# Gate, up and the sums of w_down: a written order on VectorE, ScalarE and SyncE's DMA queue

## The chip, the cores and the metric

One core of one Trainium2 chip. The metric is the device time of one execution in microseconds (us). The kernel before takes 1179.62 us, the median of three executions (1178.41 to 1179.66).

## The reference, cut to what matters

One layer with 1024 frames of width 1024: a mixer of attention and a recurrent unit, and then the part that the change touches, a SwiGLU of inner width 2816:

```python
h2 = rmsnorm(x, norm2_g[l])
x = x + (jax.nn.silu(h2 @ w_gate[l]) * (h2 @ w_up[l])) @ w_down[l]
```

All of it is float32. The kernel writes every float32 operand as a high and a low part, and every product as three products of those parts.

## The kernel before, in words

**Where the change lies.** The mixer comes first, and the diff does not touch it. After the second norm the kernel has h2, transposed, as four blocks B11, B12, B21 and B22 (512 of width by 512 frames). The 2816 columns of w_gate and of w_up are taken in 11 pairs of 128-column tiles. The first pair is multiplied the plain way, in eight blocks of 24 matmuls (`classic`). The other ten pairs are 20 steps (`Step`), in turn gate and up: g1, u1, g2, u2, up to g10, u10. A step is a 2x2 block product after Strassen and Winograd with seven products, 0 to 6, of 12 matmuls each, 84 in all. Its weight-side operands are sums of blocks of the raw weights (S1 to S4, on GpSimd in `Step.sums`), and its other side are B blocks or the sums T1 to T4 (`t_sums`, `t_split`), which are made once ahead of the steps.

**What follows each product.** `Step.run` issues product i, then what takes its result out of PSUM, then `after(i)`. Products 0, 1 and 2 are copied out by ScalarE (L1140: `pug` in a gate step, `puu` in an up step). Products 3 to 6 go through `result`: in a gate step VectorE adds a copy to the PSUM bank (L1133) and ScalarE applies silu (L1135); in an up step VectorE adds (L1128) and multiplies with the gate (L1130). Three PSUM banks, x, z and w, serve a step: products 0, 2, 4 and 6 go to x, so product 4 can't start before ScalarE has copied x after product 2, and product 6 not before VectorE has read x after product 4. Gate and up steps use different banks. `after(i)` then makes operand i of the next step (`make`, `split`): ScalarE rounds to the high part (L72, such as `au14h`: step u1, operand 4), VectorE subtracts it for the low part (L73, `au14l`). Raw weights (`graw`, `uraw`) are loaded one step ahead of that (`load_raw`).

**w_down's sums.** The last stage multiplies with w_down, also after Strassen and Winograd, in seven products P1 to P7 of 11 accumulation steps (77 steps, operands `d00h` to `d761l`, L1382). It needs four sums of w_down's blocks, and these are made in the shadow of gate and up. For each of 11 tiles f, `load_wd` issues two DMAs from ScalarE's queue (L1048, `act.dma_start`, 512 KB each) into one tile of 128 x 4 x 512 (`wd`, a pool with one buffer), `sum_wd` makes four subtractions of 128x512 on VectorE (L1054), and after the fourth SyncE's queue writes the tile to the scratch tensor `td` (L1056, 1 MB). The next `load_wd` reuses the one buffer, so its DMA waits for that write. In the code `load_wd(f)` stands after product 13f-1 and the sums 7 to 10 products behind it, so f comes every 13 products.

**What sets the order.** The framework's scheduler orders each engine's instructions by its own model of time and by priority: nothing in gate and up binds it to the written order. An engine issues its instructions in that order, one behind the other, and a DMA's issue is an instruction of the engine whose queue it uses. All other DMAs (raw weights, spills `gd` and `sd` of the gated product, `td`, and the loads of the last stage `dv`, `dx`, `dh..`, `dk`, `dq`, `dr`, `ds` in `load_d`, L1210) are issued by SyncE. In the last step, u10, `after` calls `end_step`, which issues the first loads of the last stage and makes its first operands.

Of the kernel before, what the change touches and what calls it, by code (L numbers as in the profile page):

```python
# [9 lines left out]
F32 = mybir.dt.float32  # L10
# [9 lines left out]
P = 128  # L20
# [14 lines left out]
def hymba_layer(ctx: ExitStack, tc: tile.TileContext, x, norm1_g, w_in, q_norm_g, k_norm_g, b_f,  # L35
# [5 lines left out]
    act, dve, pool, pe, sp = nc.scalar, nc.vector, nc.gpsimd, nc.tensor, nc.sync  # L41
# [9 lines left out]
    def slot(tag, name, dt=F32, shape=(P, 1024)):  # L51
        return sl.tile(list(shape), dt, tag=tag, name=name)
# [7 lines left out]
    def bank(tag, name):  # L60
        return psp.tile([P, 512], F32, tag=tag, name=name, bufs=BANKS[tag])
# [3 lines left out]
    def any_bank(name, tags=("st", "st", "st", "o", "o", "mx")):  # L65
        cyc[0] += 1
        return bank(tags[cyc[0] % len(tags)], name)

    def split(src, h, l, gain=None):

        if gain is None:
            act.copy(out=h, in_=src)  # L72
            dve.tensor_sub(out=l, in0=src, in1=f32(h))  # L73
        else:
            act.activation(out=h, in_=src, func=AF.Copy, scale=gain)
            dve.scalar_tensor_tensor(out=l, in0=src, scalar=gain, in1=f32(h), op0=ALU.mult, op1=ALU.subtract)  # L76

    def rstd(out_t, ss, n, neghalf):

        dve.tensor_scalar(out=out_t, in0=ss, scalar1=1.0 / n, scalar2=EPS, op0=ALU.mult, op1=ALU.add)  # L80
        pool.tensor_tensor(out=out_t, in0=out_t, in1=neghalf, op=ALU.pow)
# [240 lines left out]
    def sumsq_to_rstd(sq, dst, n, ps, b0=0, b1=NB):  # L322
        for b in range(b0, b1):
            pe.matmul(ps[:, b:b + 1], sq[:, b * P:(b + 1) * P], ones1[:, 0:1], start=True, stop=True)
        rstd_newton(dst[:, b0:b1], ps[:, b0:b1], n, b1 - b0)

    with tc.tile_pool(name="pp", bufs=1) as pp:
# [114 lines left out]
        for g, src in ((0, w_a), (1, w_x)):  # L442
            for o in range(2):
                sp.dma_start(out=wgr[o * HD:(o + 1) * HD, g, :, o * HD:(o + 1) * HD],
                             in_=src[0].rearrange("(t two) d e -> two d t e", two=2)[o])
# [397 lines left out]
    for h in range(H):  # L843
# [13 lines left out]
        steps = att_steps(h)  # L857
# [43 lines left out]
    NPR = NFT // 2  # L901
# [24 lines left out]
    def load_raw(nm, n):  # L926
        src = w_gate if nm == "g" else w_up
        for j in range(2):
            raw = slot("v%d" % (2 * (nm == "u") + j), f"{nm}raw{n}{j}", F32, (P, 4, 256))
            sp.dma_start(out=raw, in_=src[0, j * 512:(j + 1) * 512, n * 256:(n + 1) * 256].rearrange("(k p) c -> p k c", p=P))  # L930
            raws[nm, j] = raw
# [53 lines left out]
    with tc.tile_pool(name="nz", bufs=1) as nz:  # L985
        g2 = nz.tile([P, D], F32, name="g2")
        sp.dma_start(out=g2, in_=norm2_g[0:1, :].broadcast_to([P, D]))
        for b in range(4, NB):
            sp.dma_start(out=x1[b], in_=x1d[b * P:(b + 1) * P, :])
        x2d = dr.tile([S, D], F32, name="x2d")  # L990

        def norm2_block(b):
            xn = nz.tile([P, D], F32, tag="xn", name=f"x2n{b}", bufs=1)
            act.activation(out=xn, in_=x1[b], func=AF.Square, accum_out=ss2[:, b:b + 1])
            rstd(rs2[:, b:b + 1], ss2[:, b:b + 1], D, neghalf[:, 0:1])
            dve.scalar_tensor_tensor(out=xn, in0=x1[b], scalar=rs2[:, b:b + 1], in1=g2, op0=ALU.mult, op1=ALU.mult)
            ts = slice((b % 4) * P, (b % 4 + 1) * P)
            for kg in range(4):
                ps = any_bank(f"t2{b}{kg}", A4)
                for j in range(2):  # L1000
                    kc = kg * 2 + j
                    pe.transpose(ps[:, j * P:(j + 1) * P], xn[:, kc * P:(kc + 1) * P], ident)
                h, l = (t[kg % 2][:, :, ts] for t in B[kg // 2, b // 4])
                split(ps[:, :256].rearrange("p (k t) -> p k t", k=2), h, l)

        for b0, nb in ((0, 2), (2, 1), (3, 1), (4, 1), (5, 1), (6, 1), (7, 1)):
            groups = [(any_bank(f"wa{b}{half}", B4), b, half) for b in range(b0, b0 + nb) for half in range(2)]
            mm_out(groups)
            if b0 in (0, 3):
                sumsq_to_rstd(sqA, rsA, AW, bank("tr", f"ssA{b0}"), *((0, 4) if b0 == 0 else (4, 8)))  # L1010
            for ps, b, half in groups:
                dve.scalar_tensor_tensor(out=x1[b][:, hs(half)], in0=ps, scalar=rsA[:, b:b + 1], in1=x1[b][:, hs(half)], op0=ALU.mult, op1=ALU.add)
            for b in range(b0, b0 + nb):
                sp.dma_start(out=x2d[b * P:(b + 1) * P, :], in_=x1[b])
            for b in ((0, 1) if b0 == 2 else (b0 - 1,) if b0 else ()):
                norm2_block(b)
            if b0 == 5:
                load_raw("g", 0)
                load_raw("u", 0)
            if b0 == 6:  # L1020
                classic_ops(0)
        g_tiles(0)


        seq = ("o1 g00 N7 ta0 g10 rw tb0 ta1 g11 tb1 ta2 g01 tb2 ta3 mk0 u00 tb3 mk1 u01 mk2 u10 sp0 mk3 mk4 u11 mk5 sp1 "
               "mk6 wd0").split()
        i7 = seq.index("N7")
        for q in seq[:i7]:
            classic_ops(1) if q == "o1" else classic(q[0], int(q[1]), int(q[2]), ops0)
        norm2_block(7)  # L1030

    tz = ctx.enter_context(tc.tile_pool(name="tz", bufs=1))
# [5 lines left out]
    ND = NFT // 2  # L1038
    TD = {"T1": 0, "T3": 1, "T4": 2, "T2": 3}
    td = dr.tile([ND, P, 4, 512], F32, name="td")  # L1040
    sd = dr.tile([ND, P, 512], F32, name="sd")
    wds = {}

    def load_wd(f):
        wds[f] = wd = tz.tile([P, 4, 512], F32, tag="wd", name=f"wd{f}", bufs=1)
        for i in range(2):
            rows = slice((ND * i + f) * P, (ND * i + f + 1) * P)
            act.dma_start(out=wd[:, 2 * i:2 * i + 2, :], in_=w_down[0, rows, :].rearrange("p (j c) -> p j c", j=2))  # L1048

    def sum_wd(f, m):  # L1050

        wd = wds[f]
        o, a, b = ((0, 1, 0), (1, 3, 1), (3, 3, 0), (2, 2, 3))[m]
        dve.tensor_sub(out=wd[:, o, :], in0=wd[:, a, :], in1=wd[:, b, :])  # L1054
        if m == 3:
            sp.dma_start(out=td[f], in_=wd)  # L1056

    T1 = slots4("q", "T1")
    T2 = slots4("k", "T2")
# [8 lines left out]
    def t_sums(k):  # L1068

        if k % 2 == 0:  # L1070
            t = tz.tile([P, 4, 512], F32, tag="wd", name=f"ts{k}", bufs=1)
            u = [t[:, i, :] for i in range(4)]
        else:
            u = [temp(f"ts{k}{i}") for i in range(4)]
        for i, blk_ in enumerate((B11, B12, B21, B22)):
            h, l = ck(blk_, k)
            dve.tensor_add(out=u[i], in0=f32(h), in1=f32(l))
        for o, x_, y_ in ((0, 1, 0), (1, 3, 1), (3, 3, 0), (2, 2, 3)):
            dve.tensor_sub(out=u[o], in0=u[x_], in1=u[y_])
        tsum[k] = u  # L1080
# [74 lines left out]
    for q in seq[i7 + 1:]:  # L1155
# [4 lines left out]
        elif q == "rw":  # L1160
            load_raw("g", 1)
            load_raw("u", 1)
            steps = [Step(nm, n) for n in range(1, NPR) for nm in "gu"]
# [91 lines left out]
    def end_step(i):  # L1255
        if i == 0:
            load_d("A11", 0, places("v2", "v3"))
            load_d("B11", 0, places("v0", "v1"))
            load_d("A11", 4, places("x3"))
            load_d("B11", 4, places("x2"))  # L1260
            for n in range(3):
                source(n)
        elif i == 1:
            load_d("A11", 6, places("hE"))
            load_d("B11", 6, places("hD"))
        elif i == 2:
            last["k0"] = places("k0")
            load_d("A11", 10, last["k0"][:1])
            load_d("B11", 10, last["k0"][1:])
            load_d("B21", 0, places("hC"))  # L1270
        elif i == 3:
            load_d("A12", 0, places("k1", "k2", "k3", "q0"))
        elif i == 4:
            load_d("B21", 8, places("q2"))
        elif i == 5:
            load_d("A12", 8, places("q1"))
            load_d("S3", 0, places("r0", "r1", "r2", "r3"))
        if i < 6:
            operand(i // 2, i % 2)

    for k, st in enumerate(steps):
        def after(i):
            f, m = divmod(7 * k + i + 1, 13)
            if 0 <= f < ND:
                if m == 0:
                    load_wd(f)
                elif 7 <= m < 11:
                    sum_wd(f, m - 7)
            if k + 1 < len(steps):
                steps[k + 1].make(i)  # L1290
            else:
                end_step(i)
        if st.n + 1 < NPR:
            load_raw(st.nm, st.n + 1)
        st.run(after)

    sq2 = cp.tile([P, 2, 512], F32, tag="sqacc", name="sq2")
    hf = places("hF")
# [31 lines left out]
    for n, (nm, a_, b_, pos) in enumerate(dsteps):  # L1330
# [16 lines left out]
        if nm == "P6" and 7 <= pos < 11:  # L1347
            b = pos - 7
# [19 lines left out]
        if nm == "P4" and 4 <= pos < 8:  # L1368
            b = pos - 4
# [8 lines left out]
        for b in range(4):  # L1378
# [9 lines left out]
            u = at({"P1": x2t[0, 0], "P2": x2t[0, 0], "P3": val.get("a"), "P7": val.get("q"), "P4": val.get("q")}[nm], b)  # L1388
# [30 lines left out]
```

## Time and profile before

| what | us |
|---|---|
| three executions, median | 1179.62 |
| lowest, highest | 1178.41, 1179.66 |
| the profiled execution, its own time | 1180.42 |
| its span, first to last instruction | 1178.6 |
| TensorE busy in the span | 1144.2 |
| VectorE, ScalarE, GpSimd busy | 770.9, 536.2, 173.0 |

Span and busy times are of the profiled execution. TensorE's busy time is modelled from the ends of pipelined matmuls, so a small idle time of it is more telling than a large busy one. The mean granted clock of TensorE over the span is 0.991 of full speed.

### The profile page before, as it was taken

How to read it: one execution, taken by the hardware profiler on the slowest of the kernel's cores; microseconds unless marked ns; L12 is line 12 of the kernel's file. 1: busy time of each engine (PE TensorE's matmuls, PEld its weight loads, DVE VectorE, ACT ScalarE, POOL GpSimd, SP SyncE). 2: the span in 40 equal slices, each digit the busy share in tenths (PEclk: the TensorE clock that was granted, in tenths of full speed). 3: DMA queues.
4: the chain of work that ended last, by engine and by line, in shares of the span. 5: the costliest groups of instructions: out<-in, count | busy, mean ns of one | idle time of the engine just before them, and what ended most of it. 6: DMA issues, size and time to landing. Idle time of an engine off the chain costs nothing.

```text
span 1178.6 us, 16612 instructions
## 1 busy us (share of the span) xinstructions
PE 1144.2 (97%) x6148; PEld 969.8 (82%) x6148; DVE 770.9 (65%) x1358; ACT 536.2 (45%) x989; POOL 173.0 (15%) x152
## 2 busy tenths in 40 slices
PE   8999999998999898999989999999999999999998
PEld 6988999996888787788867887888888888888887
DVE  6436858768788775779765666654434446679693
ACT  7437867325465454454333333333333334444442
POOL 1000010012010201110522223232222100000000
PEclk9999999998999999999999999999999999999999
DMA  6021111134665466551447555533222389842320
GB/s 251 22 60 46 38 37 37 30 73 107 163 163 148 130 150 201 198 177 37 161 169 265 208 180 195 185 128 107 72 72 90 125 312 327 298 144 97 97 82 36
DMA packets 94937, 159.70 MB, mean 136 GB/s; under 512 B 13112, under 2 KB 56232, under 8 KB 93448
## 3 DMA queue, kind: packets, MB, share of 16 engines
q1 hardware_dynamic: 91688, 147.11, 39.5%
q10 hardware_dynamic: 3168, 11.54, 2.9%
q8 instruction: 48, 0.79, 0.3%
q14 instruction: 33, 0.27, 0.1%
HBM read 103.41 MB, written 38.63 MB: 121 GB/s over the span
## 4 chain that ended last, share of the span: by engine, by line
PE 75%; DVE 11%; DMA 8%; ACT 2%; issue 2%; POOL 1%; SPq 1%; ACTq 0%; DVEq 0%; POOLq 0%
PE P L1382 18%; PE Pu L965 13%; PE Pg L965 11%; PE pbv L399 4%; PE pax L383 4%; PE pbq L399 3%; PE o L727 3%; PE pag L383 3%; PE fl L812 3%; DMA td<-wd 3%; PE pbk L399 3%; PE wa L890 2%; DMA wd<-in_w_down_dram 2%; DVE wd L1054 1%; PE mx L298 1%
## 5 line engine op out<-in xcount | busy, mean ns | idle before, releaser
L713 ACT ACTIVATE pt<-st 128x512 f32<-128x512 f32 (+1 forms) x96 | 47.8, 508 | 56.8 <-PE st L708 28.5
L718 DVE TENSOR_TENSOR ringl<-pt,ringh 128x512 fp32r<-128x512 f32 (+2 forms) x96 | 58.1, 620 | 7.0 <-ACT ringh L715 5.6
L1054 DVE TENSOR_TENSOR wd<-wd 128x512 f32<-128x512 f32 x44 | 43.9, 998 | 26.0 <-DMA wd<-in_w_down_dram 25.6
L301 DVE TENSOR_REDUCE nm<-mx 128x1 f32<-128x512 f32 (+2 forms) x96 | 51.3, 551 | 13.0 <-PE mx L300 7.3
L812 PE MATMUL fl<-worec,rech 128*128 128x256 f32 x256 | 54.7, 295 | 1.9 <-DVE ql L76 1.5
L812 PEld LDWEIGHTS fl<-worec,rech 128*128 128x128 f32 x256 | 43.7, 198 | 4.4 <-DVE ql L76 1.9
L1133 DVE TENSOR_TENSOR g<-Pg,pug 128x512 f32<-128x512 f32 x30 | 20.7, 689 | 29.9 <-PE Pg L965 29.9
L705 PE MATMUL st<-set 128*128 128x512 f32 (+1 forms) x96 | 36.4, 381 | 3.6 <-ACT pt L713 3.5
L727 PE MATMUL o<-ringh,vh 128*128 128x512 f32 (+1 forms) x96 | 38.5, 401 | 0.0
L727 PE MATMUL o<-ringl,vh 128*128 128x512 f32 (+1 forms) x96 | 35.1, 366 | 2.1 <-DVE ringl L718 2.1
L812 PE MATMUL fl<-worec,recl 128*128 128x256 f32 x128 | 37.1, 290 | 0.0
L1128 DVE TENSOR_TENSOR puu<-Pu,puu 128x512 f32<-128x512 f32 x30 | 20.7, 689 | 23.3 <-PE Pu L965 23.3
L727 PE MATMUL o<-ringh,vl 128*128 128x512 f32 (+1 forms) x96 | 34.6, 360 | 0.3 <-POOL vl L679 0.3
L1135 ACT ACTIVATE g<-g 128x512 f32<-128x512 f32 x30 | 18.9, 632 | 31.0 <-DVE g L1133 21.5
L679 POOL TENSOR_TENSOR vl<-vn,vh 128x256 fp32r<-128x256 f32 x16 | 13.6, 854 | 113.5 <-ACT vh L678 113.5
L1097 POOL TENSOR_TENSOR S1g<-graw,graw 128x512 f32<-128x512 f32 x10 | 14.8, 1480 | 104.6 <-DVE T L73 34.5
L509 POOL TENSOR_TENSOR sqR<-sqR,i 128x1024 f32<-128x1024 f32 x3 | 7.2, 2405 | 152.1 <-ACT i L508 152.1
L464 DVE SCALAR_TENSOR_TENSOR xc<-xr,vcol,xc 128x1023 f32<-128x1023 f32 (+2 forms) x12 | 15.4, 1280 | 18.6 <-ACT xc L462 18.5
L298 PE MATMUL mx<-set,qms 67*128 67x512 f32 (+2 forms) x72 | 25.9, 388 | 1.3 <-DVE nm L301 1.2
L715 ACT CAST ringh<-pt 128x512 fp32r<-128x512 f32 (+1 forms) x48 | 26.4, 549 | 1.6 <-PE o L727 0.8
L890 PE MATMUL wa<-wah,atth 128*128 128x512 f32 x64 | 25.8, 403 | 0.7 <-ACT wah L72 0.7
L812 PEld LDWEIGHTS fl<-worec,recl 128*128 128x128 f32 x128 | 25.3, 198 | 0.6
(2174 smaller groups left out, 3996.8 us busy)
## 6 DMA issues: line engine op xcount, KB each, us to landing
graw<-in_w_gate_dram SPq DMA_DIRECT2D x22, 512.0 KB
uraw<-in_w_up_dram SPq DMA_DIRECT2D x22, 512.0 KB
wd<-in_w_down_dram ACTq DMA_DIRECT2D x22, 512.0 KB
gd<-g SPq DMA_DIRECT2D x22, 512.0 KB
td<-wd SPq DMA_DIRECT2D x11, 1024.0 KB
xt<-in_x_dram SPq DMA_DIRECT2D x8, 512.0 KB
set<-qh SPq DMA_DIRECT2D x16, 256.0 KB
xp<-in_x_dram SPq DMA_DIRECT2D x32, 128.0 KB
```

The source lines that it names most:

```text
L298: pe.matmul(ps[:, :w], qm[:67, qb * P:(qb + 1) * P], kb[:67, j0 * P:j0 * P + w], start=True, stop=not diag)
L301: dve.tensor_reduce(out=nm[:, ch * 8 + qb:ch * 8 + qb + 1], in_=ps[:, :nk], axis=AX.X, op=ALU.max, negate=True)
L383: pe.matmul(ps[g][:, :n], a, r, start=(kc == 0 and m == 0), stop=(kc == KC - 1 and m == 2))
L399: pe.matmul(ps[g][:, :n], a, r, start=(kc == 0 and m == 0), stop=(kc == KC - 1 and m == 2))
L713: act.activation(out=pt[:, off:], in_=ps[:, off:], func=AF.Exp)
L718: dve.tensor_sub(out=pl[:, off:], in0=pt[:, off:], in1=f32(ph[:, off:]))
L727: pe.matmul(ot[:, off:], a[:, j * VW:j * VW + P], r[:, off:], start=(j == 0 and m == 0), stop=(j == jmax and m == 2))
L812: pe.matmul(ps[:, :256], a, r, start=(n == 0), stop=(n == 11))
L890: pe.matmul(ps, a, r[:, hs(half)], start=(kc == 0 and m == 0), stop=(kc == 3 and m == 2))
L965: pe.matmul(ps, a[:, k, :], chunk(b, k), start=first and m == 0, stop=last and m == 11, skip_group_check=more)
L1054: dve.tensor_sub(out=wd[:, o, :], in0=wd[:, a, :], in1=wd[:, b, :])
L1382: pe.matmul(ps, x_[:, bs], y_, start=(begin and m == 0), stop=(end and m == 2))
```

## The change

Four things change. (1) The loop over the 20 steps is put under a manual schedule for VectorE, ScalarE and SyncE: on these three the instructions of the loop stand in the order in which the code writes them. (2) w_down's sums go by 22 units q of 256 columns, with two buffers: `load_wd(q)` stands after product 6q-3, the four sums (128x256 now) after products 6q+4 to 6q+7, and the write of 512 KB to `td` behind the fourth. The first two units are loaded ahead of the loop (`wd0 wd1`). (3) These loads are issued by SyncE, not by ScalarE. (4) `t_sums`, which borrows the same buffers, takes two tiles of half the size.

```diff
-               "mk6 wd0").split()
+               "mk6 wd0 wd1").split()
...
-    def load_wd(f):
-        wds[f] = wd = tz.tile([P, 4, 512], F32, tag="wd", name=f"wd{f}", bufs=1)
+    def load_wd(q):
+
+        f, cs = q // 2, slice((q % 2) * 256, (q % 2 + 1) * 256)
+        wds[q] = wd = tz.tile([P, 4, 256], F32, tag="wd", name=f"wd{q}", bufs=2)
         for i in range(2):
             rows = slice((ND * i + f) * P, (ND * i + f + 1) * P)
-            act.dma_start(out=wd[:, 2 * i:2 * i + 2, :], in_=w_down[0, rows, :].rearrange("p (j c) -> p j c", j=2))
-
-    def sum_wd(f, m):
-
-        wd = wds[f]
+            sp.dma_start(out=wd[:, 2 * i:2 * i + 2, :], in_=w_down[0, rows, :].rearrange("p (j c) -> p j c", j=2)[:, :, cs])
+
+    def sum_wd(q, m):
+
+        wd = wds[q]
         o, a, b = ((0, 1, 0), (1, 3, 1), (3, 3, 0), (2, 2, 3))[m]
         dve.tensor_sub(out=wd[:, o, :], in0=wd[:, a, :], in1=wd[:, b, :])
         if m == 3:
-            sp.dma_start(out=td[f], in_=wd)
+            sp.dma_start(out=td[q // 2][:, :, (q % 2) * 256:(q % 2 + 1) * 256], in_=wd)
...
-            t = tz.tile([P, 4, 512], F32, tag="wd", name=f"ts{k}", bufs=1)
-            u = [t[:, i, :] for i in range(4)]
+            t = [tz.tile([P, 4, 256], F32, tag="wd", name=f"ts{k}{i}", bufs=2).rearrange("p (a b) c -> p a (b c)", a=2) for i in range(2)]
+            u = [t[i // 2][:, i % 2, :] for i in range(4)]
...
-    for k, st in enumerate(steps):
-        def after(i):
-            f, m = divmod(7 * k + i + 1, 13)
-            if 0 <= f < ND:
-                if m == 0:
-                    load_wd(f)
-                elif 7 <= m < 11:
-                    sum_wd(f, m - 7)
...
+    with tc.manual_schedule(engines={mybir.EngineType.DVE, mybir.EngineType.Activation, mybir.EngineType.SP}):
+        for k, st in enumerate(steps):
+            def after(i):
+                e = 7 * k + i
+                for q in range(2 * ND):
+                    if e == 6 * q - 3 and q >= 2:
+                        load_wd(q)
+                    elif 0 <= e - (6 * q + 4) < 4:
+                        sum_wd(q, e - 6 * q - 4)
```

**The order in three places.** The first is ScalarE, from the end of step g1 (copies `pug`, silu into `g`) with the operands of u1 between. Before:

```order
L1140 COPY pug_6408<-Pg_6404 128x512
L72 CAST au13h<-uraw_6130 128x512
L1048 DMA wd_6668<-in_w_down_dram 128x1024
L1135 ACTIVATE g_6409<-g_6409 128x512
L72 CAST au14h<-S3u_6426 128x512
L1048 DMA wd_6668<-in_w_down_dram 128x1024
L1135 ACTIVATE g_6410<-g_6410 128x512
```

And after the change:

```order
L1142 COPY pug_6415<-Pg_6411 128x512
L72 CAST au12h<-S2u_6432 128x512
L1137 ACTIVATE g_6416<-g_6416 128x512
L72 CAST au13h<-uraw_6131 128x512
L1137 ACTIVATE g_6417<-g_6417 128x512
L72 CAST au14h<-S3u_6433 128x512
L1137 ACTIVATE g_6416<-g_6416 128x512
```

The two loads of `wd` are gone from ScalarE, and each operand's cast stands behind the result of its product, where it stood ahead of it.

The second is VectorE in step u1, where operands of g2 are made. Before:

```order
L73 TENSOR_TENSOR ag21l<-S1g_6565,ag21h 128x512
L1054 TENSOR_TENSOR wd_6942<-wd_6942 128x512
L73 TENSOR_TENSOR ag22l<-S2g_6566,ag22h 128x512
L1128 TENSOR_TENSOR puu_6549<-Pu_6548,puu_6549 128x512
L73 TENSOR_TENSOR ag23l<-graw_6402,ag23h 128x512
L1130 TENSOR_TENSOR g_6409<-g_6409,puu_6549 128x512
```

And after the change:

```order
L73 TENSOR_TENSOR ag21l<-S1g_6575,ag21h 128x512
L73 TENSOR_TENSOR ag22l<-S2g_6576,ag22h 128x512
L1130 TENSOR_TENSOR puu_6558<-Pu_6557,puu_6558 128x512
L1132 TENSOR_TENSOR g_6416<-g_6416,puu_6558 128x512
L1056 TENSOR_TENSOR wd_6402<-wd_6402 128x256
L73 TENSOR_TENSOR ag23l<-graw_6409,ag23h 128x512
```

The sum of `wd` stood ahead of the additions that empty the banks of u1; now it is half as wide, of the second unit (loaded ahead of the loop), and stands behind them.

The third is SyncE's queue at the turn to the last step, u10, with the loads of the last stage (`dv`, `dx`: first operands A11 and B11 of P1; `ds`: A22). Before:

```order
L1210 DMA dv_9204<-in_w_down_dram 128x2x512
L953 DMA gd<-g_8758 128x1024
L953 DMA gd<-g_8759 128x1024
L1210 DMA dv_9205<-in_w_down_dram 128x2x512
L1210 DMA dv_9200<-gd 128x2x512
L1210 DMA dx_9208<-gd 128x2x512
L1210 DMA dx_9210<-in_w_down_dram 128x2x512
L1210 DMA ds_9370<-gd 128x2x512
```

And after the change:

```order
L1212 DMA ds_9463<-gd 128x2x512
L1212 DMA ds_9464<-gd 128x2x512
L1058 DMA td<-wd_9088 512x1x256
L1212 DMA dv_9297<-gd 128x2x512
L1212 DMA dv_9298<-gd 128x2x512
L1212 DMA dv_9301<-in_w_down_dram 128x2x512
L1212 DMA dv_9302<-in_w_down_dram 128x2x512
L1212 DMA dx_9305<-gd 128x2x512
```

Five of the six first loads stood ahead of those of A22 and right behind the spills of u9; now all six stand behind A22's and behind the write of the last unit of `td`, which waits for its fourth sum, after product 0 of u10.

## Rows read from the trace of the kernel before

**Rows 1.** The page, busy time, share of the span, instructions: TensorE.

```profile
PE 1144.2 (97%) x6148; PEld 969.8 (82%) x6148; DVE 770.9 (65%) x1358; ACT 536.2 (45%) x989; POOL 173.0 (15%) x152
```

**Rows 2.** The chain that ended last: start, length in us, what.

```profile
946.53 19.04 PE Pu L965 x84
965.57 207.41 PE P L1382 x915
```

**Rows 3.** Instructions on the tile Pg: durations, first and last start.

```profile
L965 PEld LDWEIGHTS Pg<-B,ag10h x8: 187/188/188, 570.5 to 572.7; 128*128 128x128 f32 x8
```

**Rows 4.** Timeline of weight loads: start, us, instruction, [idle before <- releaser].

```profile
597.52 0.31 PEld L965 LDWEIGHTS Pu<-T,au12h 128*128 128x128 f32 x2 [2.62 <-ACT puu L1140]
604.90 0.30 PEld L965 LDWEIGHTS Pu<-T,au14h 128*128 128x128 f32 x2 [0.47 <-ACT puu L1140]
612.49 0.19 PEld L965 LDWEIGHTS Pu<-T4hB,au16h 128*128 128x128 f32 x1 [2.26 <-DVE puu L1128]
634.73 0.19 PEld L965 LDWEIGHTS Pg<-T4hB,ag26h 128*128 128x128 f32 x1 [3.33 <-DVE g L1133]
733.20 0.19 PEld L965 LDWEIGHTS Pu<-T4hB,au46h 128*128 128x128 f32 x1 [1.76 <-DVE puu L1128]
761.28 0.30 PEld L965 LDWEIGHTS Pu<-T,au52h 128*128 128x128 f32 x2 [1.01 <-ACT puu L1140]
```

**Rows 5.** Windows: us, busy (x instructions) by engine, clock, DMA share, GB/s.

```profile
601.00:660.00 59.00, 54.21 (x229) 43.72 (x228) 37.80 (x51) 17.26 (x30) 17.18 (x12) 0.97 0.59 214
762.00:966.00 204.00, 204.00 (x902) 168.96 (x901) 90.05 (x136) 73.93 (x127) 50.28 (x36) 1.00 0.37 123
927.00:938.00 11.00, 11.00 (x51) 9.09 (x50) 3.37 (x5) 3.94 (x7) 0.86 (x1) 1.00 0.84 285
953.00:990.00 37.00, 37.00 (x165) 30.66 (x164) 18.20 (x29) 12.86 (x23) 0.00 (x0) 1.00 0.93 330
```

**Rows 6.** Waits, 525 to 770: who for whom, us, times, longest.

```profile
DVE wd L1054 <- DMA wd<-in_w_down_dram: 25.6, 11, 7.1
...
ACT g L1135 <- DMA td<-wd: 9.5, 2, 8.1
...
ACT puu L1140 <- DMA td<-wd: 5.8, 1, 5.8
```

**Rows 7.** Timeline of ScalarE near 590.

```profile
589.91 0.33 ACTq L1048 DMA_DIRECT2D wd<-in_w_down_dram  x1
590.29 0.63 ACT L1135 ACTIVATE g<-g 128x512 f32<-128x512 f32 x1 [8.13 <-DMA td<-wd]
```

**Rows 8.** Timeline of VectorE, two sums of w_down that waited.

```profile
607.36 0.69 DVE L1054 TENSOR_TENSOR wd<-wd 128x512 f32<-128x512 f32 x1 [7.14 <-DMA wd<-in_w_down_dram]
...
626.87 0.69 DVE L1054 TENSOR_TENSOR wd<-wd 128x512 f32<-128x512 f32 x1 [4.91 <-DMA wd<-in_w_down_dram]
```

**Rows 9.** The chain again: two writes of td, 1 MB each.

```profile
598.43 4.87 DMA td<-wd
...
744.32 9.40 DMA td<-wd
```

**Rows 10.** VectorE, 128x256 once, and the 44 sums (ns least/median/most).

```profile
501.02 0.42 DVE L73 TENSOR_TENSOR B<-t,B 128x256 fp32r<-128x256 f32 x1 [0.74 <-ACT B L72]
...
L1054 DVE TENSOR_TENSOR wd<-wd x44: 676/692/1787, 574.5 to 762.0; 128x512 f32<-128x512 f32 x44
```

**Rows 11.** Timelines of SyncE and GpSimd: a raw load issued, and landed.

```profile
680.74 0.37 SPq L930 DMA_DIRECT2D uraw<-in_w_up_dram  x1
...
685.09 1.29 POOL L1097 TENSOR_TENSOR S1u<-uraw,uraw 128x512 f32<-128x512 f32 x1 [6.30 <-DMA uraw<-in_w_up_dram]
```

**Rows 12.** Timelines of VectorE, SyncE and ScalarE around the start of u10.

```profile
947.05 0.69 DVE L73 TENSOR_TENSOR au106l<-uraw,au106h 128x512 fp32r<-128x512 f32 x1 [1.91 <-ACT au106h L72]
...
931.44 0.37 SPq L1210 DMA_DIRECT2D dv<-gd  x1
...
951.83 0.62 ACT L72 CAST d01h<-dv 128x512 fp32r<-128x512 f32 x1 [1.61 <-issue]
...
955.08 0.58 ACT L1140 COPY puu<-Pu 128x512 f32<-128x512 f32 x1
```

More of the change, by code (lines that the diff above doesn't have):

```diff
@@ L1279, in end_step @@
             operand(i // 2, i % 2)
-    for k, st in enumerate(steps):
-        def after(i):
-            f, m = divmod(7 * k + i + 1, 13)
-            if 0 <= f < ND:
-                if m == 0:
-                    load_wd(f)
-                elif 7 <= m < 11:
-                    sum_wd(f, m - 7)
[L1289 to L1295, printed above, removed]
+    with tc.manual_schedule(engines={mybir.EngineType.DVE, mybir.EngineType.Activation, mybir.EngineType.SP}):
[7 more added lines that the diff above has]
+                        sum_wd(q, e - 6 * q - 4)
+                if k + 1 < len(steps):
+                    steps[k + 1].make(i)
+                else:
+                    end_step(i)
+            if st.n + 1 < NPR:
+                load_raw(st.nm, st.n + 1)
+            st.run(after)
     sq2 = cp.tile([P, 2, 512], F32, tag="sqacc", name="sq2")
```

## The prediction

> **What bounds the kernel now.** I read the page first: TensorE is busy 1144.2 of 1178.6 us [rows 1], so time can come only out of what it waits for, and a faster other engine is worth nothing by itself. Next the chain that ended last: an undisturbed step of gate and up is one row of 84 matmuls in 19.04 us, and the last stage is one unbroken run of 207.41 us [rows 2]. There is nothing to win in the last stage, nor in the late steps: from 762 to 966 TensorE is busy without a gap at clock 1.00 [rows 5].
>
> So the question is what the 20 steps take beyond 20 x 19.04 = 380.8 us. The first weight load of g1 stands at 570.5 [rows 3] and the last stage begins at 965.57 [rows 2]: 395.1 us. **The excess is 14.3 us**, and all of it lies ahead of 762. The timeline of the weight loads names it: six waits of 2.62, 0.47, 2.26, 3.33, 1.76 and 1.01 us, 11.45 in all, each ended by ScalarE's or VectorE's work on a bank [rows 4]. The other 2.8 us are matmuls that ran slower behind those waits: the granted clock is 0.97 between 601 and 660 against 1.00 later [rows 5].
>
> Why were the two engines late? The list of waits: VectorE stood 25.6 us in 11 waits for w_down's loads, ScalarE 9.5 and 5.8 us for the write of td [rows 6]. The timelines show the mechanism on both. ScalarE's next load of wd can't be issued before the one buffer is written out, and everything behind that issue stands still: silu 8.13 us, up to 590.29 [rows 7], and the copies of u1 stand behind it; TensorE waits at 597.52 and 604.90 [rows 4]. On VectorE a sum stands ahead of the additions that empty the bank and waits 7.14 us for its data at 607.36, another 4.91 at 626.87 [rows 8]; TensorE waits at 612.49 and 634.73 [rows 4]. The last of the 44 sums starts at 762.0 [rows 10], and the last gap ends at 761.28 [rows 4]: no sums, no gaps.
>
> **The change part by part.**
>
> Loads off ScalarE. 22 issues of 0.33 us [rows 7] leave it, which is off the path; what counts is that no silu, copy or cast stands behind a wait for td any more. The three waits that ScalarE ended are 2.62 + 0.47 + 1.01 = 4.1 us [rows 4], and with their share of the slow matmuls (14.3 / 11.45 = 1.25) 5.1 us.
>
> The Trainium skill ("DMA: Bandwidth & Descriptors", Issuing engines are not separate DMA queues) says that starting DMAs from several engines saves only the sequencer's time to start them, which is small. By that rule moving the loads to SyncE is worth little and those 5.1 us would stay. The rows disagree for this kernel: it is the wait ahead of the issue, 8.13 us, that ScalarE pays for.
>
> Units of 256 with two buffers. A unit is loaded after product 6q-3 and first used after 6q+4: seven products, 19.04 us. Even the slowest write of 1 MB ahead of it, 9.40 us [rows 9], and a raw load's 4.35 us from issue to landing (680.74 to 685.09) [rows 11] make 13.8. VectorE should find its data there, and the 2.26 + 3.33 + 1.76 = 7.35 us that it ended [rows 4], 9.2 with the slow share, go too. VectorE has more instructions for it: 88 sums at the 0.42 us of a 128x256 one [rows 10] are 37.0 us, where 44 at the median 0.69 are 30.4. These 6.6 us I cost at nothing: in an undisturbed step VectorE is busy 90 of 204 us [rows 5]. If that cover went, a few sums per step at 0.42 would be the price.
>
> The written order. On ScalarE and VectorE casts and low parts now stand behind the result of each product. In a gate step that makes a chain per product: add 0.69, silu 0.63, cast 0.62, subtraction 0.69 [rows 7, 8, 12] = 2.63 us, against a product of 19.04 / 7 = 2.72. It fits, and the bank that the add frees is wanted only a product later. I cost it at nothing; from above it is a few tenths per step if the links between engines add much.
>
> SyncE. It gets 44 loads of 256 KB, and 22 writes of 512 KB instead of 11 of 1 MB: 55 more issues of 0.37 us [rows 11], 20 us in 395, and it may wait for a td write ahead of each load. Behind it stand raw loads and spills. A raw load is first used a whole step and a product later, 21.8 us, and takes 4.35 [rows 11]; its two halves 8.7. So 13 us of lag cost nothing.
>
> The turn to the last stage. This is where the written order costs. The loads of the first operands of P1 stood ahead of u10: `dv` of gd was issued at 931.44 [rows 12]. Now they stand behind the last td write, which waits for au106l (947.05 + 0.69) [rows 12] and one sum of 0.42: about 948.2. ScalarE, in written order, runs copy, d00h, copy, d01h, copy; the third copy frees the bank for product 4, and stands behind d01h, which needs the third dv load, the first of B11. Four transfers of 512 KB (td, two of A11, B11), 2.1 MB, at 285 to 330 GB/s [rows 5] from about 949.5 land at 955.9 to 956.9; cast and copy, 0.62 + 0.58 [rows 12], make 957.1 to 958.1. Product 4 is due at 946.53 + 4 x 2.72 = 957.4. A lone load takes 4.35 us [rows 11], some 2.5 more than its bytes, so a landing may be up to that much later. The stall is 0 to 4 us; I take **1.0**, near the lower end, since transfers in a row hide each other's start.
>
> **The sum.** The profiled execution's own time is 1180.42 (span 1178.6 and 1.8 around it): 1180.42 - 5.1 - 9.2 + 1.0 = 1167.1. It stands 0.8 above the median of the runs, so **1166.3**.
>
> **The rivals.**
>
> 1. *Part of the early waits stays* (1173). For it: u1 comes right behind t_sums, and SyncE and VectorE still share the work; the waits of u1 are 2.62 + 0.47 + 2.26 = 5.35, 6.7 with the slow share: 1166.3 + 6.7. Against it: the releasers there all stood behind wd or td [rows 6 to 8].
> 2. *The move off ScalarE is worth nothing* (1171.4). ScalarE's three waits would stay if its copies were late for another reason than the issue ahead of them, such as the data in flight: 1166.3 + 5.1. The Trainium skill's page on DMA, cited above, would have it so. Against it: rows 7.
> 3. *The last stage starves* (1171). The six loads of dv and dx, 3.1 MB, and 0.5 MB of td come 11 us later at 330 GB/s, into a queue that was 93% busy from 953 to 990 [rows 5]. For it: all later loads shift by that. Against it: d00h to d30h are needed one after the other over 19 us, and later operands had long landed. A shift beyond the slack by 5 us gives 1171.
> 4. *SyncE's queue becomes the wait* (1186, slower). Place: the issue of a load of wd behind the td write two products (5.4 us) before. If each write takes 9.4 us [rows 9], SyncE stands 4.0 us per unit, 4.7 per step, with the raw loads behind it. It decides from 13 us per step on, as above; at 14 each of the 20 steps starts 1 us late: 1166.3 + 20. Against it: that needs three times the worst write. The Trainium skill ("DMA: Bandwidth & Descriptors", Rules for kernel authors) speaks for it: it wants 1 MiB or more per DMA, and these are halved. No run here yet shows writes in pieces of 1 KB.
> 5. *The change doesn't reach the cause* (1179.6). The waits of rows 4 would come from VectorE's load and GpSimd's, not from wd. Against it: the same steps without sums have no gap [rows 5].
>
> **How the numbers follow.** Forecast 0.73, rival 1 0.08, rival 2 0.02, rival 3 0.06, rival 4 0.05, rival 5 0.06. A measurement of this kernel can tell 0.2%, 2.4 us, from no change. Forecast and rivals 1 to 3 are faster: 0.89. Rival 5 is the same: 0.06. Rival 4 is slower: 0.05. The range: below, all 14.3 from the fastest run, 1178.41 - 14.3, some 1164.0; above, the forecast with the full 4 us of the last step is 1169.3, and rivals 2 and 3 take it to 1171.5, which leaves out rivals 1, 4 and 5, 0.19.
>
> **What the profile should show.** Right: no weight load in g1 to u9 that waits for ScalarE or VectorE; steps of 19.04 us from g1 on; no wait of ScalarE for td and hardly any of VectorE for w_down; clock 1.00 from 601 to 660; sums down to u10. In u10 d00h or d01h waits for its dv load, and product 4 perhaps for the copy behind it. Wrong: a step over 19.1 us ahead of u10, GpSimd's S1 waiting for graw or uraw, or a last stage longer than 207.4 us.

## The result, and the profile after

| | before | after |
|---|---|---|
| median of four executions, us | 1179.10 | 1166.56 |
| lowest to highest | 1178.41 to 1179.66 | 1165.24 to 1166.72 |
| profiled execution, its own time | 1180.42 | 1166.72 |
| its span | 1178.6 | 1164.9 |

The ratio is 0.9891 [0.9874, 0.9909]: the change is 12.5 us faster. The time predicted was 1166.3. One execution of the change without the order ran 1599.99 us at a mean granted clock of 0.654; it and its profile are left out below.

How the steps are measured from here on: the first weight load of g1 to the first weight load of the last stage, less the 20 x 19.04 = 380.8 us of undisturbed steps; what is left is called the steps' excess. Before, that is 570.5 [rows 3] to 965.2 (0.4 ahead of the matmul in [rows 2]), an excess of 13.9. Of the kernel after, these are two rows on tiles (duration least/median/most in ns, first and last start), the last stage and then g1:

```profile
L1386 PEld LDWEIGHTS P<-d01h,d00h x4: 188/188/188, 951.4 to 953.4; 128*128 128x128 f32 x4
L965 PEld LDWEIGHTS Pg<-B,ag10h x8: 187/188/188, 568.4 to 570.7; 128*128 128x128 f32 x8
```

951.4 - 568.4 = 383.0, an excess of **2.2 us**. So 11.7 of the 13.7 us between the two profiled executions were won in the steps; the other 2 lie ahead of g1, in work that the diff does not touch (below).

Where the steps stood still before [rows 4], the windows of the kernel after (width in us, then busy us and instructions of PE, PEld, DVE, ACT, POOL; clock; DMA share; GB/s) have no gap at all: TensorE is busy for 59.00 of 59.00 and for 373.00 of 373.00 us, at clock 1.00 where [rows 5] had 54.21 of 59 and 0.97.

```profile
601.00:660.00 59.00, 59.00 (x262) 48.84 (x261) 36.64 (x58) 20.64 (x37) 16.00 (x12) 1.00 0.50 170
568.00:941.00 373.00, 373.00 (x1647) 308.88 (x1646) 209.55 (x331) 132.72 (x235) 101.17 (x76) 1.00 0.46 153
```

What is left is in u10, two waits in the timeline of the weight loads: 0.47 us at product 5, whose first matmuls ran ahead of product 4 here, and 1.97 at product 4. They answer to [rows 4], but the releaser is now one of the last step's copies:

```profile
941.51 0.30 PEld L965 LDWEIGHTS Pu<-B,au105h 128*128 128x128 f32 x2 [0.47 <-ACT puu L1142]
944.00 0.30 PEld L965 LDWEIGHTS Pu<-T,au104h 128*128 128x128 f32 x2 [1.97 <-ACT puu L1142]
```

The chain that ended last is, as in [rows 2], the end of a step and the same unbroken 207.41 us:

```profile
944.00 7.78 PE Pu L965 x33
951.78 207.41 PE P L1386 x915
```

The busy times of the page, to be laid beside [rows 1], show that no engine has fewer instructions. TensorE has the same 6148 matmuls in 5.5 us less; part of that is the lower granted clock of before behind the waits [rows 5], the rest isn't traced. VectorE has 44 instructions and 4.2 us more:

```profile
PE 1138.7 (98%) x6148; PEld 967.0 (83%) x6148; DVE 775.1 (67%) x1402; ACT 534.8 (46%) x989; POOL 165.5 (14%) x152
```

On the tile `wd` of the kernel after, the 88 sums run from 583.1 to 932.4, where the 44 of before ran from 574.5 to 762.0 [rows 10]. In the experiments every kernel with the full gain has that spread.

```profile
L1056 DVE TENSOR_TENSOR wd<-wd x88: 409/418/1496, 583.1 to 932.4; 128x256 f32<-128x256 f32 x88
L1050 SPq DMA_DIRECT2D wd<-in_w_down_dram x44: 540/602/1485, 552.5 to 903.9; - x44
L1058 SPq DMA_DIRECT2D td<-wd x22: 562/573/596, 590.3 to 932.8; - x22
```

### The profile page after: what moved, and what is told of

It reads as the page before. It is cut to its first block, busy times and chain, and to the rows that moved or that the text cites. A ratio compares the mean times of both kernels' runs of the same rounds, so it can differ in the third digit from the quotient of the medians.

```text
span 1164.9 us, 16639 instructions
## 1 busy us (share of the span) xinstructions
PE 1138.7 (98%) x6148; PEld 967.0 (83%) x6148; DVE 775.1 (67%) x1402; ACT 534.8 (46%) x989; POOL 165.5 (14%) x152
## 5 line engine op out<-in xcount | busy, mean ns | idle before, releaser
L1056 DVE TENSOR_TENSOR wd<-wd 128x256 f32<-128x256 f32 x88 | 43.8, 498 | 0.0
L1142 ACT COPY pug<-Pg 128x512 f32<-128x512 f32 x30 | 17.6, 587 | 55.5 <-PE Pg L965 55.5
L1142 ACT COPY puu<-Pu 128x512 f32<-128x512 f32 x30 | 17.6, 587 | 45.2 <-PE Pu L965 45.2
L679 POOL TENSOR_TENSOR vl<-vn,vh 128x256 fp32r<-128x256 f32 x16 | 12.5, 791 | 112.3 <-ACT vh L678 112.3
```

The source lines that it names most:

```text
L1142: act.copy(out=(p1, p5, u1)[i], in_=ps)
```

## The experiments

The prediction had put the gain down to two parts of the change: 5.1 us to the loads that leave ScalarE, 9.2 to the units of 256 with two buffers; the written order was to be worth nothing. The rival is that the order does it, by setting the loads and sums apart. Each ratio is against the kernel before, run beside it on the same chip (its median was 1178.75 us beside the first four kernels, 1177.45 beside order and queue, early loads and the change once more, 1178.03 beside the other three), and the columns "steps" and "sums" come from one profiled execution.

| kernel | median us | ratio [95%] | steps' excess | sums, first to last start |
|---|---|---|---|---|
| written order alone | 1164.25 | 0.9879 [0.9861, 0.9898] | 0.2 | 587.0 to 950.0 |
| SyncE's queue alone | 1172.72 | 0.9949 [0.9930, 0.9967] | 8.2 | 571.4 to 746.0 |
| units and buffers alone | 1191.92 | 1.0115 [1.0092, 1.0138] | 27.2 | 571.3 to 716.1 |
| change, loads left on ScalarE | 1166.97 | 0.9901 [0.9880, 0.9921] | 1.3 | 582.2 to 931.5 |
| order and queue, 512 columns, one buffer | 1164.61 | 0.9899 [0.9870, 0.9929] | 0.0 | 587.4 to 950.0 |
| change without the order | 1191.88 | 1.0124 [1.0086, 1.0162] | 24.9 | 572.6 to 729.1 |
| order on VectorE alone | 1164.30 | 0.9895 [0.9871, 0.9919] | 0.0 | 585.5 to 949.4 |
| order on ScalarE alone | 1166.12 | 0.9911 [0.9886, 0.9937] | 0.9 | 570.5 to 930.2 |
| change, first loads of the last stage earlier | 1164.18 | 0.9890 [0.9871, 0.9909] | 0.0 | 582.9 to 932.2 |
| change once more | 1165.22 | 0.9905 [0.9884, 0.9926] | 1.4 | 582.0 to 931.3 |

### The written order alone

```diff
-    for k, st in enumerate(steps):
+    with tc.manual_schedule(engines={mybir.EngineType.DVE, mybir.EngineType.Activation, mybir.EngineType.SP}):
+        for k, st in enumerate(steps):
...
```

The body of the loop, cut here, is only indented. Everything else is the kernel before: units of 512 columns, one buffer, the loads on ScalarE.

> Only the written order; loads stay on ScalarE, in units of 512 columns with one buffer. My theory: the stalls come from where the scheduler put loads and sums, so the order alone spaces them (sums 7 products, 19 us, behind their load; the load 3 products, 8.2 us, behind the write of td, which takes 4.9 to 9.4 us): excess of the 20 steps 2 to 4 us instead of 14.3, most of it in the last step, and about 1167 to 1168. Rival, that queue and second buffer do it: ScalarE's waits for td stay at over 10 us, excess 9 us or more, 1173 or slower.

Measured: 1164.25, the whole gain. Steps from 567.8 to 948.8, an excess of 0.2. One window of it, and the sums and writes (tile `wd`):

```profile
570.00:940.00 370.00, 370.00 (x1634) 306.36 (x1633) 198.66 (x282) 133.68 (x234) 99.49 (x75) 1.00 0.44 151
```

```profile
L1054 DVE TENSOR_TENSOR wd<-wd x44: 679/684/1459, 587.0 to 950.0; 128x512 f32<-128x512 f32 x44
L1056 SPq DMA_DIRECT2D td<-wd x11: 320/339/376, 595.1 to 967.7; - x11
```

One buffer is enough, and a load on ScalarE's queue hurts nobody, once the order that the code writes (a load every 13 products, its sums 7 to 10 products later) is the order that runs. The part that the prediction costed at nothing carries all of it.

### SyncE's queue alone

```diff
-            act.dma_start(out=wd[:, 2 * i:2 * i + 2, :], in_=w_down[0, rows, :].rearrange("p (j c) -> p j c", j=2))
+            sp.dma_start(out=wd[:, 2 * i:2 * i + 2, :], in_=w_down[0, rows, :].rearrange("p (j c) -> p j c", j=2))
```

> Only the loads' queue: SyncE issues them, the scheduler orders all engines. My theory: the 5.1 us of waits that ScalarE ended go, VectorE's 9.2 stay: about 1174, and no wait of ScalarE for td. Rival, that the issuing queue is worth only its issue time: 1178 to 1180. Second rival, that SyncE's queue held by td delays raw weights: GpSimd waits for graw and uraw, 1180 or slower.

Measured: 6.0 us faster (1178.75 - 1172.72). The waits of ScalarE for `td` are gone, and TensorE has four waits in place of six (timeline of its weight loads):

```profile
594.53 0.32 PEld L965 LDWEIGHTS Pu<-T,au12h 128*128 128x128 f32 x2 [2.75 <-ACT puu L1140]
...
608.83 0.19 PEld L965 LDWEIGHTS Pu<-T4hB,au16h 128*128 128x128 f32 x1 [1.94 <-DVE puu L1128]
...
685.20 0.19 PEld L965 LDWEIGHTS Pu<-T4hB,au36h 128*128 128x128 f32 x1 [0.34 <-DVE puu L1128]
...
725.19 0.19 PEld L965 LDWEIGHTS Pu<-T4hB,au46h 128*128 128x128 f32 x1 [2.03 <-DVE puu L1128]
```

VectorE still waits, as before [rows 6]:

```profile
DVE wd L1054 <- DMA wd<-in_w_down_dram: 27.5, 13, 7.9
```

So the size of the prediction's first term, 5.1, was right for this part by itself, though not for the waits it was made of: the first of them, 2.62 us behind ScalarE's copy [rows 4], stayed with 2.75. The timelines of VectorE and ScalarE show what stands behind it now. A sum waits 7.87 us for its data, the addition into `g` stands behind the sum, ScalarE's silu waits 7.32 us for that addition, and the copies of u1 stand behind the silu:

```profile
590.52 0.69 DVE L1054 TENSOR_TENSOR wd<-wd 128x512 f32<-128x512 f32 x1 [7.87 <-DMA wd<-in_w_down_dram]
591.13 0.69 DVE L1133 TENSOR_TENSOR g<-Pg,pug 128x512 f32<-128x512 f32 x1
...
591.85 0.63 ACT L1135 ACTIVATE g<-g 128x512 f32<-128x512 f32 x1 [7.32 <-DVE g L1133]
...
593.89 0.58 ACT L1140 COPY puu<-Pu 128x512 f32<-128x512 f32 x1
```

So with the issue gone from ScalarE, VectorE's wait for the data of `wd` took its place.

### Units of 256 with two buffers alone

The change with the loads back on ScalarE and without the written order:

```diff
-            sp.dma_start(out=wd[:, 2 * i:2 * i + 2, :], in_=w_down[0, rows, :].rearrange("p (j c) -> p j c", j=2)[:, :, cs])
+            act.dma_start(out=wd[:, 2 * i:2 * i + 2, :], in_=w_down[0, rows, :].rearrange("p (j c) -> p j c", j=2)[:, :, cs])
...
-    with tc.manual_schedule(engines={mybir.EngineType.DVE, mybir.EngineType.Activation, mybir.EngineType.SP}):
+    if True:
```

> Only the units of 256 columns with two buffers; loads on ScalarE, the scheduler orders all engines. My theory: the second buffer takes part of the waits away, but the scheduler still puts sums and loads close behind each other: excess 5 to 12 us, 1170 to 1177. Rival, that the second buffer alone is what counts: excess under 2, 1166 to 1167.

Measured: 13.2 us **slower** than before. All 88 sums are done by 716: the scheduler packs the 22 units closer than the 11 were. ScalarE then stands behind the issue of a load (timeline of ScalarE; the bracket is the idle time ahead):

```profile
586.14 1.21 ACTq L1050 DMA_DIRECT2D wd<-in_w_down_dram  x2
587.48 0.62 ACT L72 CAST au13h<-uraw 128x512 fp32r<-128x512 f32 x1 [10.70 <-issue]
```

VectorE's low part of that cast waits with it, 7.53 us, and the addition that empties the bank stands behind the low part and three sums:

```profile
588.12 0.69 DVE L73 TENSOR_TENSOR au13l<-uraw,au13h 128x512 fp32r<-128x512 f32 x1 [7.53 <-ACT au13h L72]
...
590.93 0.68 DVE L1135 TENSOR_TENSOR g<-Pg,pug 128x512 f32<-128x512 f32 x1
```

TensorE waits for that bank (its weight loads):

```profile
591.66 0.29 PEld L965 LDWEIGHTS Pg<-T4hB,ag16h 128*128 128x128 f32 x1 [8.13 <-DVE g L1135]
```

This is one of nine such waits; before, there were six and the longest was 3.33 [rows 4].

### The change with its loads left on ScalarE

```diff
-            sp.dma_start(out=wd[:, 2 * i:2 * i + 2, :], in_=w_down[0, rows, :].rearrange("p (j c) -> p j c", j=2)[:, :, cs])
+            act.dma_start(out=wd[:, 2 * i:2 * i + 2, :], in_=w_down[0, rows, :].rearrange("p (j c) -> p j c", j=2)[:, :, cs])
```

> The change with the loads left on ScalarE: units of 256 with two buffers, written order. My theory: the load stands two products, 5.4 us, behind a write of 512 KB that takes about 5 us, so ScalarE hardly waits: 1166 to 1168, excess 2.5 to 4. Rival, that the move to SyncE is worth its 5.1 us under any order: 1171.

Measured: 1166.97 beside the change's 1166.56; the steps' excess is 1.3, one wait of 1.46 in u10. Under the written order the queue is worth nothing that can be measured.

### Order and queue without units; units and queue without order

Two kernels that keep two of the three parts. The first is the kernel before with both edits shown first above. The second is the change with only this:

```diff
-    with tc.manual_schedule(engines={mybir.EngineType.DVE, mybir.EngineType.Activation, mybir.EngineType.SP}):
+    if True:
```

> Written order and loads on SyncE, but units of 512 columns with one buffer. My theory: with the order the second buffer is worth nothing here: 1166 to 1167.5, excess 1 to 3 us. Rival, that the one buffer keeps VectorE waiting for its data: 1170 or slower, with VectorE waiting for w_down over 5 us.

> The change without the written order: units of 256, two buffers, loads on SyncE, the scheduler orders all engines. My theory: ScalarE free and part of VectorE's waits gone: 1168 to 1174; sums still wait for w_down on VectorE (some us in the list of waits). Rival, that order adds nothing to queue and buffers: 1164 to 1166, no wait of VectorE for w_down.

> Units of 256 on SyncE without the written order, once more for a profile at full clock: 1191, excess of the 20 steps 25 to 28 us. My theory: 22 short rounds of write, load and sums run one behind the other, all sums done by about 720, and VectorE waits over 15 us for w_down. Rival, that SyncE's queue holds the raw weights: GpSimd waits over 30 us for graw and uraw and TensorE for their operands.

Order and queue: 1164.61, excess 0.0, no wait. Units and queue: 1191.10, the median of three executions, and 1191.88 in the second run, whose profile has an excess of 24.9. The queue that by itself won 6.0 us does nothing for the crowded units. VectorE now waits 40.9 us in 15 waits, and its timeline shows how one of them reaches a bank: the addition into `g`, which empties it, stands behind sums that stand for data.

```profile
590.52 0.42 DVE L1056 TENSOR_TENSOR wd<-wd 128x256 f32<-128x256 f32 x1 [8.08 <-DMA wd<-in_w_down_dram]
...
591.52 0.88 DVE L1056 TENSOR_TENSOR wd<-wd 128x256 f32<-128x256 f32 x2 [0.57 <-DMA wd<-in_w_down_dram]
592.33 0.68 DVE L1135 TENSOR_TENSOR g<-Pg,pug 128x512 f32<-128x512 f32 x1
```

TensorE's weight load waits with it:

```profile
593.06 0.28 PEld L965 LDWEIGHTS Pg<-T4hB,ag16h 128*128 128x128 f32 x1 [8.27 <-DVE g L1135]
```

### Whose order it is

The kernel before with one engine bound at a time:

```diff
-    for k, st in enumerate(steps):
+    with tc.manual_schedule(engines={mybir.EngineType.DVE}):
+        for k, st in enumerate(steps):
```

and the same with `mybir.EngineType.Activation` alone.

> The kernel before with the written order on VectorE alone; the scheduler orders ScalarE and SyncE. My theory now: what costs is where the scheduler puts the sums and, following from that, the loads; bound to the written places on VectorE, loads follow (every 13 products), and the excess of the 20 steps is under 1.5 us: 1164 to 1166. Rival, that ScalarE's own order matters as much: its copies wait for td, excess 4 us or more, 1168 or slower.

> The kernel before with the written order on ScalarE alone (its queue issues w_down's loads, so the loads are spaced too); the scheduler orders VectorE. My theory now: spaced loads leave the sums little to wait for, so excess 0 to 3 us, 1164 to 1167. Rival, that the sums' place on VectorE decides: the scheduler still puts them right behind the load it believes to be fast, VectorE waits over 10 us for w_down, 1170 or slower.

VectorE's order alone: 1164.30, excess 0.0, and no wait of VectorE for `wd`. ScalarE's order alone: 1166.12, excess 0.9. There the loads are set apart and the sums follow them, down to 930.2, but the scheduler still puts a sum right behind its load, and VectorE waits:

```profile
DVE wd L1054 <- DMA wd<-in_w_down_dram: 21.1, 7, 5.6
```

TensorE has two waits in the steps, 0.61 and 0.56:

```profile
754.73 0.19 PEld L965 LDWEIGHTS Pu<-T4hB,au56h 128*128 128x128 f32 x1 [0.61 <-DVE puu L1128]
...
793.28 0.19 PEld L965 LDWEIGHTS Pu<-T4hB,au66h 128*128 128x128 f32 x1 [0.56 <-DVE puu L1128]
```

SyncE's queue alone had about as much (27.5 us in 13 waits), with ScalarE free of waits for `td` too, and paid 8.2 for it. So it is not the sum of VectorE's waits that costs. Either engine's order is enough, and either one spreads the 11 units over the 20 steps. Every kernel whose sums end at 930 or later has 2.2 us of excess or less, every one whose sums end by 762 has 8 or more.

That the spread by itself is the cause is argued from this table and not shown, for a written order also fixes where in a step a sum waits. VectorE's two longest waits in ScalarE's order alone end at 748.18 and 784.33:

```profile
748.18 0.69 DVE L1054 TENSOR_TENSOR wd<-wd 128x512 f32<-128x512 f32 x1 [5.37 <-DMA wd<-in_w_down_dram]
...
784.33 0.69 DVE L1054 TENSOR_TENSOR wd<-wd 128x512 f32<-128x512 f32 x1 [5.61 <-DMA wd<-in_w_down_dram]
```

Product 3 of u5 and of u6, on which the first addition of the step waits, ends only at 749.11 and 787.71, so these waits hold up no addition that is due. In the queue alone a shorter wait, 4.01 us, ends at 604.35, behind the end of product 3 of u1 at 601.87, and TensorE stands 1.94 us at 608.83:

```profile
604.35 0.69 DVE L1054 TENSOR_TENSOR wd<-wd 128x512 f32<-128x512 f32 x1 [4.01 <-DMA wd<-in_w_down_dram]
```

No kernel was run that keeps the spread and puts the waits elsewhere in the step.

### The turn to the last stage

The change with five of the six first loads of the last stage written into step g10 and not behind the last write of `td`:

```diff
         if i == 0:
-            load_d("A11", 0, places("v2", "v3"))
-            load_d("B11", 0, places("v0", "v1"))
-            load_d("A11", 4, places("x3"))
-            load_d("B11", 4, places("x2"))
+            load_d("A11", 2, places("v3"))
...
+                if k + 2 == len(steps):
+                    if i == 0:
+                        load_d("B11", 0, places("v0", "v1"))
+                    elif i == 1:
+                        load_d("A11", 4, places("x3"))
+                        load_d("B11", 4, places("x2"))
+                    elif i == 5:
+                        load_d("A11", 0, places("v2"))
```

> The change, with the first loads of the last stage (B11's and A11's for v0 to v2, x2, x3) written into step g10 and not into u10. My theory: the 2.4 us that TensorE waits in u10 are ScalarE's copy behind d01h, which waits for B11's first load; with the load a step earlier the wait goes, the excess of the 20 steps is under 0.3 us, and the time is 2.4 us below the change's: 1164.1. Rival, that the stall in u10 has another cause, such as the queue being full: no gain, 1166.5.

> The change itself, once more beside the kernel before: 1166.5, excess of the 20 steps 2.4 to 2.8 us, all in u10. It shows as well whether the 2 us ahead of gate and up that the two profiles differ by return: my theory says they are of the run, not of the change, so the stage may begin anywhere from 523 to 526 us.

Measured side by side: 1164.18 with early loads, 1165.22 for the change. The intervals overlap, so the time alone settles nothing; the traces do. ScalarE in u10 of the change (the copies and the casts `d00h`, `d01h` as in [rows 12]):

```profile
940.35 0.62 ACT L72 CAST d00h<-dv 128x512 fp32r<-128x512 f32 x1 [6.42 <-DMA dv<-gd]
940.87 0.58 ACT L1142 COPY puu<-Pu 128x512 f32<-128x512 f32 x1
...
942.85 0.62 ACT L72 CAST d01h<-dv 128x512 fp32r<-128x512 f32 x1 [1.39 <-DMA dv<-in_w_down_dram]
943.37 0.58 ACT L1142 COPY puu<-Pu 128x512 f32<-128x512 f32 x1
```

and with the early loads:

```profile
933.65 0.62 ACT L72 CAST d00h<-dv 128x512 fp32r<-128x512 f32 x1
...
936.37 0.62 ACT L72 CAST d01h<-dv 128x512 fp32r<-128x512 f32 x1
...
938.60 0.59 ACT L1142 COPY puu<-Pu 128x512 f32<-128x512 f32 x1 [1.61 <-PE Pu L965]
```

No cast waits for its load any more, the third copy waits only for TensorE, and the steps take 380.8 us, excess 0.0. The change run again has 1.4, one wait of 1.44 in the same place.

### The kernel before, once more

No edit.

> The kernel before, for a second profile: six or so waits in g1 to u5 as in the first, excess 13 to 15 us. If the 2 us by which the first profile's gate and up began later are of the run, it now begins at 522 to 524; if they are of the kernel, at 525 again.

In the profiled pair the change seemed to gain 2 us ahead of g1 too: gate and up began at 523.3, before at 525.3. A second profile of the same unchanged kernel (1175.70 us) has its first gate and up weights at 521.4 (tile `cg`):

```profile
L965 PEld LDWEIGHTS cg<-B,cg00h x16: 186/188/189, 521.4 to 541.6; 128*128 128x128 f32 x16
```

So that start moves by 4 us between two executions of one kernel (521.3 to 525.3 over 13 profiles of all the kernels here), and the 2 us need not come from the change. The steps repeat: 566.5 to 960.5, an excess of 13.2, with the same six waits (2.46, 0.44, 2.26, 3.00, 1.50 and 0.92 us).

## Why the prediction was right, and where its reasons were not

**What bounds the kernel: right.** TensorE's waits in g1 to u5 were all there was to win. They are gone, the late steps ahead of u10 and the last stage stayed as they were (207.41 us), and the time went to 1166.56 where 1166.3 stood. That it came so close is in part luck: of the 13.3 us that the sum takes off, the steps gave 11.7 in the profiled pair, and the 2 us ahead of g1 made up for the rest.

**"The written order ... I cost it at nothing": this step failed.** It is worth 14.5 us by itself (1178.75 - 1164.25), all of the excess. What the order section showed was read as rows changing places, a sum behind the additions in place of ahead of them, and its cost was asked for but not its gain. What the rows of the trace had already told is that the scheduler had the 44 sums done by 762.0 [rows 10], though the code spreads the 11 units over all 140 products of the steps. Binding the order puts them back there.

**"Units of 256 with two buffers ... 9.2 with the slow share, go too": this step failed as well.** The working (a unit loaded seven products ahead) took for granted that the written distances hold, and they hold only under the written order; then one buffer of 512 columns is as good (1164.25). Without the order the units cost 13.2 us. With it they take nothing off.

**"Loads off ScalarE", 5.1: right in size by itself, nothing in the sum.** Alone the move won 6.0 us; under the written order 1166.97 without it stands beside 1166.56 with it. The two terms were added as if each removed waits of its own, and in truth both were waits for the same crowded loads. That the sum 5.1 + 9.2 came out right is because it was all of the excess, which any cure takes; as a sum of two causes it was luck. The Trainium skill's rule ("DMA: Bandwidth & Descriptors", Issuing engines are not separate DMA queues), that issuing from another engine saves only the time to start a DMA, doesn't name the wait of an issue for its buffer. With that wait gone from ScalarE, the queue moved alone gave 0.9949 [0.9930, 0.9967]; under the written order, where ScalarE has no wait for `td` on either queue, the move is worth nothing, as the rule has it.

**The last step: mechanism right, size a little low, and not the order's alone.** Predicted 1.0 (0 to 4), measured 2.2 in one profile and 1.4 in the other, nearly all of it at product 4, behind `d01h`, as written. Two terms were mis-sized. The write of `td` at 932.81 stands 2.4 us behind the first matmul of u10 (930.42), where the prediction's numbers give 1.7 (946.53 to 948.2). From that write to `d01h` at 942.85 are 10.0 us (9.2 in the second profile), where 7.7 to 8.7 were worked out. SyncE's timeline of the change has that start:

```profile
932.81 0.57 SPq L1058 DMA_DIRECT2D td<-wd  x1
933.44 1.39 SPq L1212 DMA_DIRECT2D dv<-gd  x2
934.87 1.07 SPq L1212 DMA_DIRECT2D dv<-in_w_down_dram  x2
```

The prediction charged this stall to the written order. The order alone and order with queue, whose last write of `td` is issued at 967.7 or later, behind these loads, have 0.2 and 0.0 us; it takes the order and the units of 256 together. That transfers in a row hide each other's start, the reason given for taking 1.0, no run shows.

**VectorE's sums.** They were costed at 37.0 us for 88 beside 30.4 for 44 and hidden. Measured are 43.8 us (mean 498 ns) in the change, beside 43.9 (mean 998) before and 33.4 (mean 760) under the written order with 512 columns. Like with like, halving the sums costs 10.4 us, and it is hidden.

**The rivals.** Rival 1, waits that stay in u1: none stayed. Rival 2, the move off ScalarE worth nothing: true of the move within the change, but the waits that it was to leave behind went through the order. Rival 3, a starved last stage: 207.41 as before. Rival 4, SyncE's queue: it was held for `td` at the loads of `wd`, 39.7 us in 14, and GpSimd waited for raw weights, but nothing of it reached TensorE. The queue was held longer at a place that the rival did not name, the writes of `td`, which wait for the fourth sum: 104.1 us in 15. These are rows of the waits between 523 and 960, SyncE's and then GpSimd's:

```profile
SPq L1058 <- DVE wd L1056: 104.1, 15, 11.7
...
SPq L1050 <- DMA td<-wd: 39.7, 14, 4.5
```

```profile
POOL S1g L1099 <- DMA graw<-in_w_gate_dram: 31.2, 4, 8.8
```

The longest of these two kinds of hold, 11.7 us, stays below the 13 from which that rival was to decide. GpSimd's S1 waiting for `graw` was named a sign of being wrong, and it came, but it tells nothing here: S1 waited 14.8 us for `graw` and 14.0 for `uraw` before the change as well. Rival 5, that w_down's loads are not the cause: ruled out by the queue alone, which touches only them and won 6.0 us.

**What is left.** The kernels with order alone, order and queue, and order on VectorE stand at 1164.25 to 1164.61, early loads at 1164.18. In the steps three of these have an excess of 0.0 and the first 0.2. There is hardly more to win between g1 and the last stage by placing work; which of these versions is best, the times can't tell.

## What to carry to other kernels

When a view shows waits for a load, look first at where the loads and their users stand in time, and compare that with where the code puts them: here work for the shadow of a long stage, done in its first half, had been crowded by the scheduler. Terms of a sum that all remove the same wait must not be added without a run of each part alone; here three parts alone gave -14.5, -6.0 and +13.2 us, and together -12.5. A second buffer and smaller pieces took nothing off under the written order, which leaves room between load and use; without it they let the crowd come closer.

## What the runs showed of the hardware

**A DMA in narrow pieces takes its issuer longer.** The write of `td` from SyncE has a median of 573 ns with 512 runs of 1 KB, where 1 MB in 128 runs of 8 KB took 358; a load of `wd`, in runs of 1 KB in place of 4 KB, 602 ns in the change, 335 before. In the kernel before (tile `wd`):

```profile
L1048 ACTq DMA_DIRECT2D wd<-in_w_down_dram x22: 334/335/1467, 556.9 to 754.2; - x22
L1056 SPq DMA_DIRECT2D td<-wd x11: 338/358/497, 582.2 to 762.7; - x11
```

The prediction had taken 0.37 us for each. The median moves between kernels (412 ns for a load of 4 KB runs in the order alone, 424 in the queue alone), but the least time does not: 327 to 334 ns with runs of 4 KB and 539 to 547 with 1 KB in all profiles, on either queue.

**The long sums run beside GpSimd.** The 88 sums have a median of 418 ns and a longest of 1496. One of the longest in VectorE's timeline after the change, and GpSimd at that time:

```profile
618.43 1.50 DVE L1056 TENSOR_TENSOR wd<-wd 128x256 f32<-128x256 f32 x1
...
623.87 0.91 DVE L1056 TENSOR_TENSOR wd<-wd 128x256 f32<-128x256 f32 x1
```

```profile
618.35 1.29 POOL L1100 TENSOR_TENSOR S2g<-S1g,graw 128x512 f32<-128x512 f32 x1
623.21 1.29 POOL L1101 TENSOR_TENSOR S3g<-graw 128x512 f32<-128x512 f32 x1 [3.57 <-DVE au24l L73]
```

Both sums begin inside a GpSimd operation and end 0.28 to 0.29 us after it; the first began 0.08 us into it and took 1.50, the second 0.66 us into it and took 0.91. Of the 88 sums 14 begin inside one, all 14 end 0.28 to 0.29 us after it, and no other takes over 0.42 us. The Trainium skill ("SBUF — State Buffer", SBUF: two separate sides) says that VectorE, when both inputs are in SBUF, and GpSimd take one pair of ports in turn, each for a whole instruction. The rows agree in that no such sum ends before the GpSimd operation; that it ends 0.28 us behind, and not the 0.42 of a sum alone, says that a part of the sum runs beside it. None of it reached TensorE here.

**The kernel before varies more than the pair shows.** Over all its executions on record it lies between 1174.05 and 1180.97 us, 0.6%, and a share of that stands ahead of gate and up, as the second profile of it shows.
